# Sparse heads' attention weights: TensorE transposes replaced by DMA transposes of 16-bit planes, joined and weighted a head later

## The chip, the cores and the metric

The kernel runs on one core of a Trainium2 chip. The metric is the device time of one execution in microseconds (us). A core has five engines that work side by side, each through its own list of instructions in order: TensorE (PE in the profile; PEld is its loading of weights), VectorE (DVE), ScalarE (ACT), GpSimd (POOL) and SyncE (SP, which here issues DMAs). An engine that waits at one instruction holds up everything behind it in its list. Matrix products land in PSUM, eight banks of 128 partitions by 512 float32; everything else lives in SBUF.

## The reference

One block of a streaming encoder for 512 frames of 1024 channels, all in float32. A combined projection feeds two attention branches of 8 heads each and two gates; the branches are projected, gated, merged, put through an output projection and a layer norm; a gated feed-forward part follows. The change touches the sparse branch:

```python
def dsa_sequence(q, k, v, q_idx, k_idx, w_idx, rel_bias):      # in blocks of 128 queries
    dots = jnp.einsum('thd,sd->ths', qib, k_idx) * IDX_DIM ** -0.5
    score = jnp.einsum('th,ths->ts', wib, jax.nn.relu(dots))
    score = jnp.where(key_chunk[None, :] <= q_chunk, score, -jnp.inf)
    _, sel = lax.top_k(score, n_sel)                            # 128 keys for each query
    logits = jnp.einsum('thd,tnhd->htn', qb, k[sel]) * HEAD_DIM ** -0.5 + bias
    p = jax.nn.softmax(jnp.where(valid[None], logits, -jnp.inf), axis=-1)
    return jnp.einsum('htn,tnhd->thd', p, v[sel])
...
y_a, y_s = sparse branch, stick-breaking branch
merged = sigmoid(g_a + b0) * (y_a @ w_branch_dsa) + sigmoid(g_b + b1) * (y_s @ w_branch_sb)
```

The kernel doesn't gather keys. It computes the logits of all keys up to a query's block, adds a large penalty to those that were not chosen, and takes the softmax.

## The kernel before

Every product in float32 is made of three products in a reduced type, fp32r: a value is split into a high part (rounded to fp32r) and a low part (the rest), and high x high, high x low and low x high are summed. The weights are loaded by a `Stream` (one DMA of 512 KB on SyncE's queue per piece, three raw buffers); a piece is split by ScalarE (`whi`, L101) and by VectorE or GpSimd (`wlo`, L103).

The heads are taken in the order s0 to s7 (stick-breaking), then a0 to a7 (sparse). In pieces between the steps of the heads the main loop places "filler" matmuls, 15 at a time (`fill(GAP)`): projections of weights that will be wanted later, such as qa, ka (queries and keys of a pair of sparse heads), va (values of all sparse heads, four banks va_ps0 to va_ps3), gb and ga (gates), bs and ba (branch products). A scheduler takes the program with its own estimates of time and sets the final order on each engine; a list written once is then fixed. PSUM is shared by two pools of four banks: psA for the projections and branch products, psB for the heads' logits (l_ps, z_ps), transposes (tr_ps) and weighted values (av_ps).

A sparse head i goes through these steps. `dsa_head`: its bias window `win` comes by DMA (L474), GpSimd adds it to the scores' penalties in `bm` (L479, three blocks), TensorE makes the logits (l_ps, L490), VectorE adds `bm` and takes the row minimum into `lg` (L494, custom instruction), ScalarE takes the exponentials (L496), VectorE the reciprocals (L499) and scales `lg` by them (L502). `turn_weights`: TensorE transposes the ten 128 x 128 blocks of `lg` into three tr_ps banks (L410), ScalarE copies each bank to `pth` (high part, L414), VectorE subtracts to `ptl` (low part, L415). `weigh`: eight matmuls of the values with pth and ptl (L426: 512, 384, 256 and 128 columns, high and low), then ScalarE and VectorE add the two halves of the result (L431, L432), and every second head `finish_pair` splits it (L437, L438). The head after, i+1, has its `dsa_head` issued before head i is turned.

`proj_v` reads va_ps out: ScalarE the high parts (L252), VectorE the low parts (L253). Until all of va_ps is read out, nothing else fits into psA; the next user is the filler gb5 (lines 223 to 225).

The output projection further down, which the change leaves as it is, has a transpose of another make: ScalarE copies the two 16-bit planes of a float32 tile apart (L742), SyncE issues a DMA transpose for each (L743), ScalarE copies the planes back into one another (L750), and the high and low parts are made from that (L752, L753).

Of the kernel before, what the change touches and what calls it, by code (L numbers as in the profile page):

```python
# [11 lines left out]
F32 = mybir.dt.float32  # L12
# [32 lines left out]
OFF = {0: 0, 2: 128, 3: 512, 1: 1024}  # L45
ATT = 1280


def r32(ap):
    return ap.bitcast(F32)  # L50
# [67 lines left out]
def tile_block(ctx: ExitStack, tc: tile.TileContext, xT, xN, w_qi, w_ki, w_t, w_v, w_br, w_o, w_fi, w_fo,  # L118
# [86 lines left out]
    first = bp.tile([128, 512], F32, name="first")  # L205
# [139 lines left out]
    def idx_keys():  # L345
        ps = whole(proj_t("ki", M=72, bank=pa))
        kih = bp.tile([128, 512], F32R, tag="pt", bufs=8, name="kih")
        kil = bp.tile([128, 512], F32R, tag="pt", bufs=8, name="kil")
        wiT = bp.tile([8, 512], F32, tag="pt", bufs=8, name="wiT")
# [13 lines left out]
    def idx_scores():  # L363
        kih, kil, wi = index["k"]
        for j in (1, 2, 3):
            N = 128 * (j + 1)
            for h in range(H):
# [5 lines left out]
                rl = bp.tile([128, 512], F32, tag="pt", bufs=8, name="relu")  # L373
# [25 lines left out]

    def turn_weights(a):  # L400

        groups = (((0, 0),), ((1, 0), (3, 384)), ((2, 0),))
        pth, ptl = {}, {}
        for grp in groups:
# [7 lines left out]
            th = bp.tile([128, 512], F32R, tag="pt", bufs=8, name="pth")  # L412
            tl = bp.tile([128, 512], F32R, tag="pt", bufs=8, name="ptl")
            nc.scalar.activation(th[:, :width], ps[:, :width], AF.Copy)  # L414
            lows = nc.vector.tensor_sub(tl[:, :width], ps[:, :width], r32(th[:, :width]))  # L415
            for i, o in grp:
                pth[i] = th[:, o:o + 512 - 128 * i]
                ptl[i] = tl[:, o:o + 512 - 128 * i]
        return pth, ptl, lows.ins

    def weigh(pth, ptl, vt, h, ytmp):

        ps = pb("av_ps")
        seq = [(i, t) for i in range(NB) for t in (pth, ptl)]
        for n, (i, t) in enumerate(seq):
            nc.tensor.matmul(ps[:, 128 * i:512], vt[i][:, h].rearrange("p a d -> p (a d)"), t[i],  # L426
                             start=(n == 0), stop=(n == len(seq) - 1))
# [3 lines left out]
        nc.scalar.activation(tmp[own], ps[oth], AF.Copy)  # L431
        nc.vector.tensor_add(ytmp[own], ps[own], tmp[own])  # L432
# [39 lines left out]
    def dsa_head(q, k, h):  # L472
# [4 lines left out]
        for j in (1, 2, 3):  # L477
            N = 128 * (j + 1)
            nc.gpsimd.tensor_add(bm[:, OFF[j]:OFF[j] + N], win[:, 512 - N:512], score[j])  # L479
# [4 lines left out]
        for grp in ((3,), (0, 2), (1,)):  # L484
            ps = pb("l_ps")
            o = 0
            for j in grp:
# [4 lines left out]
                c = slice(OFF[j], OFF[j] + N)  # L492
                b = win[:, 384:512] if j == 0 else bm[:, c]
                nc.vector.tensor_tensor_reduce(out=lg[:, c], in0=ps[:, o:o + N], in1=b, scale=1.0, scalar=3.0e38,  # L494
# [642 lines left out]
```

## Time and profile before

| | us |
|---|---|
| median of 3 runs | 762.77 (762.73 to 762.90) |
| the profiled execution | 762.16 |
| span of its profile | 760.4 |
| TensorE busy | 748.6 (98%) |
| VectorE busy | 555.4 (73%) |
| ScalarE busy | 379.3 (50%) |
| GpSimd busy | 153.5 (20%) |
| TensorE clock granted, mean | 0.998 |

The profile is of one execution. The sparse heads' transposes lie between 206.1 and 321.4 us of it. In a row of a timeline the first number is the start in us from the span's start, the second the time from the first start to the last end, then engine, line, operation, output and inputs, partitions x elements, count; a bracket tells how long the engine sat idle before it and what released it. Rows of groups have the count, the busy time in us and the mean ns of one, then the idle time before it. Matmuls overlap, so the time of one row is longer than the step from its start to the next one's.

### The profile page before, as it was taken

To read this page: it belongs to the slowest core of one execution; us is meant where nothing else is said; L and a number is where in the kernel's file an instruction comes from. 1 tells how busy PE (TensorE), PEld (TensorE's weight loads), DVE (VectorE), ACT (ScalarE), POOL (GpSimd) and SP (SyncE) were. 2 spreads that over 40 slices of the span, in tenths; PEclk is the share of its full clock that TensorE was granted. 3 is DMA by queue.
4 is the path that set the end of the run, shared out by engine and by line. 5 is a ranking of instruction groups with operands and counts; after the bars stand their busy time and mean duration, and the time that the engine had idled before them with its cause. 6 is when DMAs were issued, how large, how long until landed. Compare 5 with 4: busy or idle time off the path is not lost.

```text
span 760.4 us, 9842 instructions
## 1 busy us (share of the span) xinstructions
PE 748.6 (98%) x3573; PEld 627.3 (82%) x3573; DVE 555.4 (73%) x905; ACT 379.3 (50%) x568; POOL 153.5 (20%) x160
## 2 busy tenths in 40 slices
PE   9999999999999999999999999999999999999995
PEld 7878888887888888888889888888888888888885
DVE  5569787799878585548765867766776768668995
ACT  5474756655574756835364633433443344346430
POOL 1002555426644210000111110111011101110012
PEclk9999999999999999999999999999999999999999
DMA  8445433232223324116942344544444444448632
GB/s 267 147 128 181 125 95 96 72 111 84 80 102 111 111 76 122 64 60 206 340 61 84 139 156 136 155 137 139 153 140 142 147 138 137 141 152 274 222 105 79
DMA packets 40448, 102.89 MB, mean 135 GB/s; under 512 B 10888, under 2 KB 11272, under 8 KB 40400
## 3 DMA queue, kind: packets, MB, share of 16 engines
q1 hardware_dynamic: 34672, 85.98, 35.4%
q0 software_dynamic: 3728, 11.04, 4.0%
q10 hardware_dynamic: 2000, 5.24, 2.8%
q8 instruction: 28, 0.46, 0.3%
q14 instruction: 20, 0.16, 0.1%
HBM read 88.59 MB, written 9.98 MB: 130 GB/s over the span
## 4 chain that ended last, share of the span: by engine, by line
PE 92%; DVE 5%; issue 1%; ACT 0%; POOL 0%; POOLq 0%; ACTq 0%; DVEq 0%
PE u_ps L774 5%; PE u_ps L776 5%; PE g_ps L774 5%; PE u_ps L775 5%; PE g_ps L776 5%; PE g_ps L775 5%; PE m L856 2%; PE m L854 2%; PE m L855 2%; PE av_ps L426 2%; PE ga_ps L224 2%; PE ga_ps L223 2%; PE ga_ps L225 2%; PE o_ps L704 2%; PE o_ps L703 2%; PE o_ps L705 2%
## 5 line engine op out<-in xcount | busy, mean ns | idle before, releaser
L101 ACT ACTIVATE whi<-raw 128x1024 fp32r<-128x1024 f32 (+1 forms) x124 | 124.1, 1001 | 169.5 <-PE g_ps L775 44.9
L103 DVE TENSOR_TENSOR wlo<-raw,whi 128x1024 fp32r<-128x1024 f32 (+1 forms) x105 | 120.0, 1144 | 41.3 <-ACT whi L101 40.5
L776 PE MATMUL u_ps<-x1h,wlo 128*128 128x512 f32 (+1 forms) x192 | 71.4, 372 | 0.0
L774 PE MATMUL u_ps<-x1h,whi 128*128 128x512 f32 (+1 forms) x192 | 71.3, 372 | 0.0
L775 PE MATMUL u_ps<-x1l,whi 128*128 128x512 f32 (+1 forms) x192 | 71.3, 371 | 0.0
L774 PE MATMUL g_ps<-x1h,whi 128*128 128x512 f32 (+1 forms) x184 | 69.9, 380 | 0.0
L775 PE MATMUL g_ps<-x1l,whi 128*128 128x512 f32 (+1 forms) x184 | 69.9, 380 | 0.0
L776 PE MATMUL g_ps<-x1h,wlo 128*128 128x512 f32 (+1 forms) x184 | 69.9, 380 | 0.0
L103 POOL TENSOR_TENSOR wlo<-raw,whi 128x1024 fp32r<-128x1024 f32 x19 | 45.8, 2412 | 34.5 <-ACT whi L101 34.4
L776 PEld LDWEIGHTS u_ps<-x1h,wlo 128*128 128x128 f32 x192 | 36.2, 188 | 6.3
L775 PEld LDWEIGHTS u_ps<-x1l,whi 128*128 128x128 f32 x192 | 36.2, 188 | 6.3
L774 PEld LDWEIGHTS u_ps<-x1h,whi 128*128 128x128 f32 x192 | 36.2, 188 | 6.2
L415 DVE TENSOR_TENSOR ptl<-tr_ps,pth 128x512 fp32r<-128x512 f32 (+1 forms) x48 | 27.9, 595 | 18.2 <-ACT pth L414 17.6
L776 PEld LDWEIGHTS g_ps<-x1h,wlo 128*128 128x128 f32 x184 | 34.6, 188 | 6.6
L775 PEld LDWEIGHTS g_ps<-x1l,whi 128*128 128x128 f32 x184 | 34.6, 188 | 6.5
L774 PEld LDWEIGHTS g_ps<-x1h,whi 128*128 128x128 f32 x184 | 34.6, 188 | 6.5
L797 DVE TENSOR_TENSOR t<-raw 128x512 f32<-128x512 f32 x11 | 7.6, 693 | 40.2 <-DMA raw<-in_w_fo_dram 40.2
L816 POOL MEMSET u<- 128x2 f32 x22 | 2.1, 98 | 143.7 <-ACT whi L101 99.9
L830 DVE TENSOR_TENSOR hF<-g_ps,c 128x512 f32<-128x512 f32 x22 | 15.1, 687 | 20.4 <-PE g_ps L776 20.4
L822 ACT ACTIVATE c<-c,cwt 128x512 f32<-128x512 f32 x22 | 16.0, 725 | 26.3 <-DVE c L821 26.1
L672 POOL TENSOR_TENSOR rstd<-rstd,mhalf 128x1 f32<-128x1 f32 x8 | 7.6, 951 | 106.0 <-DVE rstd L671 106.0
L414 ACT ACTIVATE pth<-tr_ps 128x512 fp32r<-128x512 f32 (+1 forms) x48 | 23.9, 520 | 9.8 <-PE tr_ps L410 6.8
(566 smaller groups left out, 2055.9 us busy)
## 6 DMA issues: line engine op xcount, KB each, us to landing
raw<-in_w_fi_dram SPq DMA_DIRECT2D x44, 512.0 KB, 3.3
raw<-in_w_t_dram SPq DMA_DIRECT2D x32, 512.0 KB, 3.4
raw<-in_w_fo_dram SPq DMA_DIRECT2D x26, 512.0 KB, 4.2
raw<-in_w_br_dram SPq DMA_DIRECT2D x8, 512.0 KB, 3.3
raw<-in_w_o_dram SPq DMA_DIRECT2D x8, 512.0 KB, 4.2
raw<-in_w_v_dram SPq DMA_DIRECT2D x7, 512.0 KB, 3.9
raw_b<-in_w_fo_dram SPq DMA_DIRECT2D x6, 512.0 KB, 4.2
s_t<-t POOLq DMA_DIRECT2D x11, 256.0 KB, 2.3
```

The source lines that it names most:

```text
L101: nc.scalar.activation(hi[:, :w], t[:, :w], AF.Copy)
L103: self.done[key] = eng.tensor_sub(lo[:, :w], t[:, :w], r32(hi[:, :w])).ins
L223: nc.tensor.matmul(ps[:M], wh[:, c], xh[k], start=(k == 0), stop=False)
L224: nc.tensor.matmul(ps[:M], wh[:, c], xl[k], start=False, stop=False)
L225: nc.tensor.matmul(ps[:M], wl[:, c], xh[k], start=False, stop=(k == KC - 1))
L414: nc.scalar.activation(th[:, :width], ps[:, :width], AF.Copy)
L415: lows = nc.vector.tensor_sub(tl[:, :width], ps[:, :width], r32(th[:, :width]))
L426: nc.tensor.matmul(ps[:, 128 * i:512], vt[i][:, h].rearrange("p a d -> p (a d)"), t[i], start=(n == 0), stop=(n == len(seq) - 1))
L774: nc.tensor.matmul(ps[:, c], wh[:, kc], x1h[:, k, c], start=(k == 0), stop=False)
L775: nc.tensor.matmul(ps[:, c], wh[:, kc], x1l[:, k, c], start=False, stop=False)
L776: nc.tensor.matmul(ps[:, c], wl[:, kc], x1h[:, k, c], start=False, stop=(k == KC - 1))
L822: nc.scalar.activation(c, c, AF.Gelu_apprx_tanh, bias=cwt[:, f, 3:4])
```

## The change

Sparse heads no longer use TensorE for their transposes. Stick-breaking heads still do.

- `send_planes`: once `lg` is scaled, ScalarE copies its odd 16-bit halves and VectorE its even ones (1280 each) into the memory of this head's own `bm`, which is read for the last time before that. SyncE issues two DMA transposes into `pl`. There is one buffer `pl` for all heads.
- `join_planes`: ScalarE copies the odd plane from `pl` into `back`, VectorE the even one; ScalarE makes `pth` of all 1280 columns, VectorE `ptl`. Both copies are issued after the next head's last exponential and last minimum.
- `weigh` comes a head later: head i is weighted after head i+1's logits are issued, just before head i+1's own planes are joined. The column order in `lg` is new (SOFF), so the transposed blocks of one block of keys lie three blocks apart and are read with a stride. Block 0's 512 columns take two pairs of matmuls (384 and 128), so ten matmuls a head.
- `pth` and `ptl` have one buffer of 1280 columns each now, for the stick-breaking heads too, where there were eight of 512 columns. Other tiles that used those eight move to other memory.

```diff
+SOFF = {1: 0, 0: 256, 2: 384, 3: 768}
...
-    first = bp.tile([128, 512], F32, name="first")
+    first = bp.tile([128, 512], F32, tag="pl", bufs=1, name="first")
...
-                rl = bp.tile([128, 512], F32, tag="pt", bufs=8, name="relu")
+                rl = bp.tile([128, 512], F32, tag=("keep", "av", "yt")[h % 3], bufs=2, name="relu")
...
+    def turned():
+        return (bp.tile([128, ATT], F32R, tag="th", bufs=1, name="pth"),
+                bp.tile([128, ATT], F32R, tag="tl", bufs=1, name="ptl"))
...
+    def halves16(t):
+        return t.bitcast(U16).rearrange("p (c two) -> p two c", two=2)
+
+    def send_planes(lg, bm):
+
+        src = halves16(lg)
+        own = bm[:, 0:ATT].bitcast(U16).rearrange("p (a c) -> p a c", a=2)
+        pl = bp.tile([128, 2, ATT // 128, 128], U16, tag="pl", bufs=1, name="pl")
+        nc.scalar.activation(own[:, 1], src[:, 1], AF.Copy)
+        nc.vector.tensor_copy(own[:, 0], src[:, 0])
+        for a in (0, 1):
+            nc.sync.dma_start_transpose(pl[:, a], own[:, a])
+        return pl
+
+    def join_planes(pl):
+
+        back = bp.tile([128, ATT], F32, tag="back", bufs=1, name="back")
+        got = pl.rearrange("p a b c -> p a (b c)")
+        nc.scalar.activation(halves16(back)[:, 1], got[:, 1], AF.Copy)
+        nc.vector.tensor_copy(halves16(back)[:, 0], got[:, 0])
+        th, tl = turned()
+        nc.scalar.activation(th, back, AF.Copy)
+        nc.vector.tensor_sub(tl, back, r32(th))
+        h, l = (t.rearrange("p (s c) -> p s c", c=128) for t in (th, tl))
+        parts = [(i, o, h[:, c], l[:, c]) for i, o, c in
+                 ((0, slice(128, 512), slice(0, 9, 3)), (0, slice(0, 128), slice(2, 3)),
+                  (1, slice(128, 512), slice(1, 9, 3)), (2, slice(256, 512), slice(5, 9, 3)),
+                  (3, slice(384, 512), slice(9, 10)))]
+        return parts
...
-        return lg
+        return send_planes(lg, bm), None, up.ins, low.ins
...
-        return sb_head(*args) if w == "s" else (dsa_head(*args),)
+        return sb_head(*args) if w == "s" else dsa_head(*args)
...
+    pair, joined = {}, None
     for i, (w, h) in enumerate(heads):
-        following = start_head(i + 1) if i + 1 < len(heads) else (None,)
+        following = start_head(i + 1) if i + 1 < len(heads) else ()
         fill(GAP)
...
+        else:
+            ends = following[2:]
+            if joined is not None:
+                added = values_of(*joined)
+                ends = ends or added
+            fill(GAP)
+            with tc.issue_after(ends[0]), tc.issue_after(ends[1]):
+                parts = join_planes(weights[0])
+            joined = parts, w, h
         fill(GAP)
         weights = following
+    fill(GAP)
+    values_of(*joined)
     fill(9999)
```

The order on VectorE around the read-out of va, before the change. The rows begin with the first sparse head's last scaling. lg_2102 and its mn_2103 are those of head a1; va0 to va3 are the values; ptl_2151 is a0's; ISA is the custom minimum.

```order
L502 TENSOR_SCALAR lg_1969<-lg_1969,rs_1972 128x512
L103 TENSOR_TENSOR wlo_36_2089<-raw_36_2086,whi_36_2088 128x1024
L494 ISA lg_2102,mn_2103<-l_ps_2111,win_2095 128x128
L494 ISA mn_2103 128x1
L432 TENSOR_TENSOR yst3_1917<-av_ps_2058,avt_2067 64x512
L494 ISA lg_2102,mn_2103<-l_ps_2120,bm_2098 128x256
L494 ISA mn_2103 128x1
L253 TENSOR_TENSOR va0_2207<-va_ps0_1945,va0_2207 128x8x64
L253 TENSOR_TENSOR va1_2210<-va_ps1_1946,va1_2210 128x8x64
L415 TENSOR_TENSOR ptl_2151<-tr_ps_2145,pth_2150 128x512
```

The same place on VectorE after the change, from a0's even plane on. lg_2075 is now head a1's, back_2144 is a0's joined tile, pl_1969 its landing buffer.

```order
L436 COPY bm_1937<-lg_1941 128x1280
L532 ISA lg_2075,mn_2076<-l_ps_2084,win_2068 128x128
L532 ISA mn_2076 128x1
L532 ISA lg_2075,mn_2076<-l_ps_2093,bm_2071 128x256
L532 ISA mn_2076 128x1
L469 TENSOR_TENSOR yst3_1889<-av_ps_2031,avt_2040 64x512
L104 TENSOR_TENSOR wlo_36_2062<-raw_36_2059,whi_36_2061 128x1024
L446 COPY back_2144<-pl_1969 128x1280
L532 ISA lg_2075,mn_2076<-l_ps_2084,bm_2071 128x384
L532 ISA mn_2076 128x1
L254 TENSOR_TENSOR va0_2206<-va_ps0_1917,va0_2206 128x8x64
L254 TENSOR_TENSOR va1_2209<-va_ps1_1918,va1_2209 128x8x64
```

The copy back from the landing buffer (L446) and a1's last minimum stand ahead of va0's low half, which stood right behind a1's third minimum; a0's low part, which was subtracted bank by bank, comes once and behind va1.

The order on GpSimd at the same place, before the change; bm_1965 and bm_2098 are the bias sums of a0 and a1, score3 the scores of the last block of queries.

```order
L103 TENSOR_TENSOR wlo_34_1952<-raw_34_1949,whi_34_1951 128x1024
L103 TENSOR_TENSOR wlo_35_2043<-raw_35_2040,whi_35_2042 128x1024
L479 TENSOR_TENSOR bm_1965<-win_1962,score3_370 128x512
L479 TENSOR_TENSOR bm_2098<-win_2095,score3_370 128x512
L475 MEMSET win_2256 64x64
```

And after the change, where bm_1937 is a0's, bm_2071 a1's.

```order
L104 TENSOR_TENSOR wlo_34_1924<-raw_34_1921,whi_34_1923 128x1024
L517 TENSOR_TENSOR bm_1937<-win_1934,score3_370 128x512
L517 TENSOR_TENSOR bm_2071<-win_2068,score3_370 128x512
L104 TENSOR_TENSOR wlo_35_2016<-raw_35_2013,whi_35_2015 128x1024
L513 MEMSET win_2166 64x64
```

The subtraction for the weights of gb5 (wlo_35) has moved from ahead of the two last bias sums to behind them.

On SyncE's queue, after the change, the DMA transposes stand between the loads (L72, weights) and the bias windows (L512); before the change the same loads stood there without them. pl_1969, pl_2103 and pl_2201 are a0's, a1's and a2's.

```order
L512 DMA win_2166<-s_win 128x512
L72 DMA raw_38_2218<-in_w_t_dram 128x1024
L438 DMA_TRANSPOSE pl_1969<-bm_1937 128x10x128 x2
L512 DMA win_2303<-s_win 128x512
L72 DMA raw_39_2266<-in_w_t_dram 128x1024
L512 DMA win_2492<-s_win 128x512
L72 DMA raw_40_2347<-in_w_t_dram 128x1024
L438 DMA_TRANSPOSE pl_2103<-bm_2071 128x10x128 x2
L72 DMA raw_41_2399<-in_w_t_dram 128x1024
L438 DMA_TRANSPOSE pl_2201<-bm_2169 128x10x128 x2
```

The loads of weights raw_39 to raw_41 now stand behind a head's transposes, which leave only when that head's planes are copied and the landing buffer has been read.

More of the change, by code (lines that the diff above doesn't have):

```diff
@@ L411, in turn_weights @@
                 width = max(width, o + 512 - 128 * i)
[L412 to L415, printed above, removed]
+            w = slice(base, base + width)
+            nc.scalar.activation(th[:, w], ps[:, :width], AF.Copy)
+            lows = nc.vector.tensor_sub(tl[:, w], ps[:, :width], r32(th[:, w]))
@@ L423, in weigh @@
+    def weigh(parts, vt, h, ytmp):
         ps = pb("av_ps")
-        seq = [(i, t) for i in range(NB) for t in (pth, ptl)]
-        for n, (i, t) in enumerate(seq):
-            nc.tensor.matmul(ps[:, 128 * i:512], vt[i][:, h].rearrange("p a d -> p (a d)"), t[i],
+        seq = [(i, o, t) for i, o, th, tl in parts for t in (th, tl)]
+        for n, (i, o, t) in enumerate(seq):
+            dst = ps[:, o] if len(t.shape) == 2 else ps[:, o].rearrange("p (s c) -> p s c", c=128)
+            nc.tensor.matmul(dst, vt[i][:, h].rearrange("p a d -> p (a d)"), t,
@@ L596, in tile_block, with values_of @@
     fill_until("qs1", "ks1")
+    def values_of(parts, w, h):
+        if h % 2 == 0:
+            pair[w] = bp.tile([128, 512], F32, tag="yt", bufs=2, name=f"y{w}t{h//2}")
+        fill_until(f"v{w}")
+        ends = weigh(parts, vals[w], h, pair[w])
+        if h % 2 == 1:
+            (ys if w == "s" else ya).append(finish_pair(pair[w], f"y{w}{h//2}"))
+        return ends
+    pair, joined = {}, None
     for i, (w, h) in enumerate(heads):
-        following = start_head(i + 1) if i + 1 < len(heads) else (None,)
+        following = start_head(i + 1) if i + 1 < len(heads) else ()
         fill(GAP)
-        pth, ptl, lows = turn_weights(weights[0])
-        if len(following) == 2:
-            with tc.issue_after(lows):
-                scan = sb_sticks(*following)
-            with tc.issue_after(scan):
-                select_some(ROUNDS[i])
-        fill(GAP)
-        if h % 2 == 0:
-            ytmp = bp.tile([128, 512], F32, tag="yt", bufs=2, name=f"y{w}t{h//2}")
-        fill_until(f"v{w}")
-        weigh(pth, ptl, vals[w], h, ytmp)
-        if h % 2 == 1:
-            (ys if w == "s" else ya).append(finish_pair(ytmp, f"y{w}{h//2}"))
+        if w == "s":
+            parts, lows = turn_weights(weights[0])
+            if len(following) == 2:
+                with tc.issue_after(lows):
+                    scan = sb_sticks(*following)
+                with tc.issue_after(scan):
+                    select_some(ROUNDS[i])
+            fill(GAP)
+            values_of(parts, w, h)
+        else:
[7 more added lines that the diff above has]
+            joined = parts, w, h
         fill(GAP)
         weights = following
+    fill(GAP)
+    values_of(*joined)
     fill(9999)
```

36 lines of the change are left out of this document (19 added, 17 removed).

## The prediction

> **What bounds the kernel now.** I read the page's busy shares first, then the chain that ended last, then TensorE's waits over the whole run, and only then the stage of the sparse heads, in windows.
>
> ```profile
> PE 748.6 (98%) x3573; PEld 627.3 (82%) x3573; DVE 555.4 (73%) x905; ACT 379.3 (50%) x568; POOL 153.5 (20%) x160
> PE 92%; DVE 5%; issue 1%; ACT 0%; POOL 0%; POOLq 0%; ACTq 0%; DVEq 0%
> PE idle_ps L200 <- DVE idle L197: 1.2, 1, 1.2
> PE dot_ps L371 <- ACT relu L374: 1.0, 1, 1.0
> PE va_ps L244 <- DVE ka1b L318: 0.9, 1, 0.9
> PE gb_ps L223 <- DVE va L253: 0.5, 1, 0.5
> 205.00:253.00 48.00, 47.47 (x236) 39.70 (x235) 37.83 (x72) 29.04 (x58) 20.84 (x19) 1.00 0.33 106
> ```
>
> TensorE bounds the kernel: it is busy for 98% and carries 92% of the chain, and its named waits add up to 3.6 us. So a matmul taken out is worth its full start-to-start time, as long as nobody makes TensorE wait. The last line is the stage from the first sparse transpose until head a4 (columns: window, length, then busy time of PE, PEld, DVE, ACT, POOL, then clock, DMA share, GB/s). VectorE works 37.83 of 48 us there, ScalarE 29.04. The cover is not wide: VectorE has some 10 us free in the very stage that the change loads. And the wait of gb_ps for va on VectorE shows the place where TensorE is already just caught.
>
> **a) The transposes that go: -8.7 us.**
>
> ```profile
> L410 PE MATMUL tr_ps<-ident,lg 128*128 128x128 f32 x80 | 12.3, 272 | 0.0
> 119.44 1.09 PE tr_ps L410 x10
> ```
>
> The first row counts them (80, ten a head); its 272 ns overlap one another and are not the price. The second is a piece of the chain: ten transposes advance it by 1.09 us, 0.109 each. 80 x 0.109 = 8.7; I leave 8.6 to 9.1 for their neighbours.
>
> **b) Narrower products: +0.2 us.** Block 0's 512 columns become 384 and 128, hi and lo, so 16 more matmuls.
>
> ```profile
> 319.31 0.34 PE L426 MATMUL av_ps<-pth,va 128*128 128x384 f32 x1
> 319.49 0.40 PE L225 MATMUL ga_ps<-xh,wlo 128*128 128x512 f32 x1
> 320.79 0.22 PE L426 MATMUL av_ps<-pth,va 128*128 128x128 f32 x1
> 320.85 0.27 PE L426 MATMUL av_ps<-ptl,va 128*128 128x128 f32 x1
> 210.88 0.39 PE L224 MATMUL gb_ps<-xl,whi 128*128 128x512 f32 x1
> 211.11 0.40 PE L225 MATMUL gb_ps<-xh,wlo 128*128 128x512 f32 x1
> ```
>
> Start to start 384 columns take 0.18 and 128 take 0.06, together 0.24; a 512-column product takes 0.23 (the last two rows). 16 x 0.01 = 0.2, between 0 and 0.5, as strided operands may cost a little and are not in this trace.
>
> **What the new path costs its engines.** The output projection of this kernel already sends 16-bit planes through DMA transposes, so most prices stand in the trace, for 1024 columns; the sparse heads have 1280, a factor of 1.25.
>
> ```profile
> L742 ACT ACTIVATE own<-r 128x1024 uint16<-128x1024 uint16 x6 | 6.0, 1047 | 8.2 <-DVE r L677 8.2
> L750 ACT ACTIVATE back<-got 128x1024 uint16<-128x1024 uint16 x6 | 7.7, 1358 | 5.5 <-DMA got<-own 5.5
> L743 SPq DMA_TRANSPOSE got<-own x6: 1233/1288/1353, 381.7 to 402.0; - x6
> DMA to landing us min/median/max: 3.1/3.2/4.9
> L752 ACT ACTIVATE x1h<-back x3: 1060/1061/1062, 389.2 to 406.6; 128x1024 fp32r<-128x1024 f32 x3
> L753 DVE TENSOR_TENSOR x1l<-back,x1h 128x1024 fp32r<-128x1024 f32 x3 | 3.7, 1221 | 1.6 <-ACT x1h L752 1.6
> L415 DVE TENSOR_TENSOR ptl<-tr_ps,pth 128x512 fp32r<-128x512 f32 (+1 forms) x48 | 27.9, 595 | 18.2 <-ACT pth L414 17.6
> L414 ACT ACTIVATE pth<-tr_ps 128x512 fp32r<-128x512 f32 (+1 forms) x48 | 23.9, 520 | 9.8 <-PE tr_ps L410 6.8
> ```
>
> Per head ScalarE gives up 23.9/16 = 1.49 us and takes on 1.31 (odd plane out), 1.70 (back) and 1.33 (pth): +2.85. VectorE gives up 27.9/16 = 1.74 and takes on ptl at 1.53 and two 16-bit copies of 1280. Such a copy is not in the trace of before. Half the subtraction's price, 0.76, is the low bound (half the bytes, and one source), the subtraction itself, 1.53, the high one; I take 1.1, the middle: +1.99 a head. SyncE's queue takes two issues of 1.29 x 1.25 = 1.6, one after the other; behind them stand the next loads of weights and of the bias window. A load behind them is up to 3.2 us later; with three raw buffers I cost that at nothing, and it would come to at most those 3.2 where a buffer is used as it lands.
>
> **c) The first join stands ahead of va's evacuation: +6.5 us.** On ScalarE and on VectorE the copies back for head a0 (L445, L446) now come before va0 is read out (L253, L254). gb5 needs the bank that this frees; the four va_ps fill all of that pool. VectorE's work while TensorE runs on becomes one serial walk: scaling, plane copies, two DMAs, copy back, va0.
>
> ```profile
> 204.57 0.17 DVE L499 RECIPROCAL rs<-sm 128x4 f32<-128x4 f32 x1
> 204.78 1.28 DVE L502 TENSOR_SCALAR lg<-lg,rs 128x128 f32<-128x128 f32 x4
> 201.40 2.53 POOL L479 TENSOR_TENSOR bm<-win,score 128x512 f32<-128x512 f32 x2 [0.36 <-DVE score L391]
> 240.69 2.52 POOL L103 TENSOR_TENSOR wlo<-raw,whi 128x1024 fp32r<-128x1024 f32 x1
> 212.91 3.81 POOL L479 TENSOR_TENSOR bm<-win,score 128x256 f32<-128x256 f32 x3 [1.08 <-DVE mn L494]
> 215.41 2.39 DVE L502 TENSOR_SCALAR lg<-lg,rs 128x128 f32<-128x128 f32 x4
> 237.98 5.51 DVE L502 TENSOR_SCALAR lg<-lg,rs 128x128 f32<-128x128 f32 x4
> 203.96 0.69 DVE L494 CUSTOM_DVE_ANT_0 lg<-l_ps,bm 128x512 f32<-128x512 f32 x1 [0.54 <-POOL bm L479]
> 209.80 1.29 DVE L253 TENSOR_TENSOR va<-va_ps,va 128x512 fp32r<-128x512 f32 x2 [1.21 <-ACT va L252]
> 210.55 0.50 PE L223 MATMUL gb_ps<-xh,whi 128*128 128x512 f32 x1 [0.53 <-DVE va L253]
> ```
>
> The scaling took 1.28 at 204.78 with GpSimd idle, 2.39 and 5.51 beside GpSimd's adds and subtractions; at 215.41 it ended 1.1 us after GpSimd's adds did (217.8 against 216.7). In the changed order GpSimd's wlo_35 stands behind the two bm adds, so it runs from 203.9 to 206.4, right beside this scaling (its first reader is gb5's third matmul, so its own lateness costs nothing). The scaling then ends at about 207.5 rather than 206.1. ScalarE's odd plane is out at 208.8; VectorE first does a1's pending minimum (0.69 and a short read), then its plane, until about 209.3. The even plane is the first sent: issue at 209.3, landing 3.2 later at 212.5, the odd one 1.6 behind, 214.1, and the copies back wait for both. Copy back 1.1, a1's next minimum 0.6, va0's low half 0.65 (1.29 for two), and gb5 starts at about 216.7 with its hop. Unhindered it would start at 210.55 - 0.53 (its old wait) - 1.09 (a0's transposes) + 0.81 (six l_ps products of a2 that now stand ahead, 512, 128 and 256 columns in pairs) = 209.7. Wait 7.0, less the 0.5 that it replaces: **+6.5**. Low bound: no GpSimd beside the scaling (-1.4), landing at 3.1, second issue at 1.3, copy at 0.76: +4.0. High bound: landing 4.9 (+1.7) and one copy held by GpSimd's next adds (+1.1): +9.3.
>
> What the Trainium skill says to this: "SBUF — State Buffer", section "SBUF: two separate sides", calls the port pair that VectorE shares with GpSimd an exclusive lock, so that one engine waits for the other's whole instruction. The rows at 204.78, 215.41 and 237.98 agree with it. By that rule the two plane copies could each also wait for a GpSimd instruction, 1 to 2.5 us more by the rows of L479 and L103, which would lead to the high end of c).
>
> **d) The later joins, a1 and a2, until a4: +3.5 us.** There is one landing buffer, so a head's DMAs wait for the join before it, and GpSimd's bias sums for the head after next wait until the planes have left their tile. VectorE carries for three heads 3 x 1.99 = 6.0 us more, ahead of the keys for the next pair:
>
> ```profile
> 249.62 0.69 DVE L318 TENSOR_TENSOR ka2b<-ka_ps,ka2b 64x512 fp32r<-64x512 f32 x1
> 253.35 0.96 PE L490 MATMUL l_ps<-ka2a,qa2a 128*128 128x512 f32 x5
> ```
>
> The keys end at 250.3 and TensorE uses them at 253.35, a margin of 3.0 us. TensorE also comes earlier, by 30 transposes, 3.3 us. With no slack used at all the stall would be 6.0 + 3.3 - 3.0 = 6.3; it is 0 if VectorE's 10 free us of the 48 take all of it. Those gaps lie partly where the new work cannot run (it waits for DMAs), so I take a little over the middle, 3.5. ScalarE's 3 x 2.85 = 8.6 fit into its 19 free us and are costed at nothing; without that cover they would come on top.
>
> **e) After the last head: +0.4 us.** a7's join hides behind ga5 and the first branch products, which no longer need it for more than 4 us; 0 to 1.5 if the landing is at its slowest.
>
> **Sum** against the profiled execution, 762.16 us (span 760.4 and 1.8 around it): -8.7 + 0.2 + 6.5 + 3.5 + 0.4 = +1.9, so 764.1. The median of the runs shown is 0.6 higher, 762.77, so the forecast is **764.7 us**.
>
> **The rivals.** *The clock falls in the pause* (0.13). For it:
>
> ```profile
> 1.18 4.02 PE idle_ps L200 x9
> ```
>
> At the start, after idling, nine matmuls take 4.02 us, 0.447 each, twice the 0.23 of later ones of 512 columns. If a pause of 7 us brings that state back, 4 us at half speed cost 2.1: 766.8. Against it: the page's clock row stands at its highest digit even there, and those matmuls may differ for their type. The Trainium skill, "TensorE: Matmul & The Clock Gate", section "HAM oscillation — how this bites in real kernels", tells of such a gate, with idle gaps above about 3.4 us closing it. No wait of this trace is that long; the longest has 1.2.
>
> *The joins break even* (0.27). c) stands but VectorE finds room for the joins, d) = 0: 764.7 - 3.5 = 761.2. For it: 10 free us on VectorE, and a stalled TensorE lets others catch up. Against it: the scaling of 5.51 us at 237.98 shows how little is sure there.
>
> *The transposes' time is kept* (0.17), the other side: VectorE and ScalarE reach va early because the planes leave at once, c) at its low bound 4.0, d) and e) nothing: -8.7 + 0.2 + 4.0 = -4.5, 758.3. It decides if gb5's first matmul starts before 214.2. For it: the uncontended scaling of 1.28; against it: GpSimd's subtraction, now placed beside that scaling.
>
> That the change leaves the transposes in place can be excluded: their instructions are gone from the order.
>
> **How the numbers follow.** The forecast has 0.43, on its own 762.8 to 766.6 (d from 1.6 to 5.4). A measurement here can tell about 0.2%, 1.5 us. Faster: all of the last rival and half of the break-even, 0.17 + 0.13 = 0.30. Same, 761.2 to 764.3: 0.14 of break-even and 0.15 of the forecast, 0.29. Slower: 0.28 and the clock's 0.13, 0.41. The range leaves out a little over half of the last rival and the worst of c) with the clock: 759.0 to 768.5.
>
> **What would show it.** No tr_ps in the sparse stage, and 8.7 us less busy time on TensorE; a wait of gb_ps for va of 5 to 9 us near 210, and in it VectorE waiting at L446 for the landing; l_ps of a4 waiting for the keys by 1 to 6 us; L540 of a0 near 2.7 us rather than 1.28; matmuls after the pause at 0.23, not 0.45. I am wrong if gb5 starts by 212, if VectorE's 16-bit copies take over 1.6, or if the time went where no wait is named here: weights that arrive late because the DMA issues of 1.6 us stand ahead of them in SyncE's queue.

## The result and the profile after

| | before | changed |
|---|---|---|
| median, us | 762.75 (762.51 to 762.90) | 767.64 (767.26 to 768.12) |
| the profiled execution, us | 762.16 | 767.37 |
| span of its profile, us | 760.4 | 765.6 |
| TensorE clock granted, mean | 0.998 | 0.993 |

The changed kernel is slower by 4.9 us, a ratio of 1.0066 with a 95% interval of 1.0053 to 1.0078. First the page's busy shares and the chain that ended last:

```profile
PE 745.0 (97%) x3509; PEld 622.2 (81%) x3509; DVE 568.1 (74%) x905; ACT 399.1 (52%) x568; POOL 155.5 (20%) x160
PE 60%; ACT 4%; DVE 2%; issue 1%; DMA 1%; POOL 0%; POOLq 0%; ACTq 0%; DVEq 0%
```

The 64 fewer matmuls are there (80 transposes less, 16 products more), but TensorE's busy time fell by 3.6 us only. Its part of the chain reads 60% where it was 92%, but the two can't be compared: followed back from the end, this chain stops at 242.4 us, so its shares add up to 68% and not to a whole. What it does show is that from 242 to 259 and from 295 to 331 us it lies on ScalarE, VectorE and DMAs. TensorE's waits say where (who waited, for whom, us in total, times, longest):

```profile
PE va_ps L245 <- DVE ka1b L319: 4.2, 1, 4.2
PE gb_ps L224 <- DVE va L254: 2.0, 1, 2.0
PE av_ps L463 <- ACT pth L448: 2.0, 1, 2.0
PE l_ps L528 <- DVE ka2a L318: 1.1, 1, 1.1
```

The dearest wait, 4.2 us for the keys ka1b, stands at 188 to 192 us, where the last stick-breaking heads run and no plane has been sent: the first DMA transpose comes at 210.7. Before, the same wait had 0.9. Two more things are in TensorE's timeline and in the windows around it (length, then busy us of PE, PEld, DVE, ACT, POOL, then clock, DMA share, GB/s):

```profile
192.32 0.76 PE L245 MATMUL va_ps<-whi,xh 128*128 128x512 f32 x1 [4.20 <-DVE ka1b L319]
192.89 0.63 PE L246 MATMUL va_ps<-wlo,xh 128*128 128x512 f32 x1
193.31 0.63 PE L247 MATMUL va_ps<-whi,xl 128*128 128x512 f32 x1
...
195.80 0.39 PE L245 MATMUL va_ps<-whi,xh 128*128 128x512 f32 x1
196.03 0.40 PE L246 MATMUL va_ps<-wlo,xh 128*128 128x512 f32 x1
```

```profile
192.00:195.40 3.40, 3.08 (x7) 2.48 (x8) 3.30 (x11) 0.83 (x3) 2.41 (x3) 0.54 0.00 0
195.40:200.00 4.60, 4.60 (x25) 3.93 (x24) 4.46 (x12) 2.06 (x5) 2.39 (x1) 0.97 0.00 0
332.00:335.40 3.40, 3.40 (x10) 2.63 (x10) 1.68 (x2) 0.00 (x0) 0.00 (x0) 0.53 0.18 43
```

After the wait the products start 0.43 us apart instead of 0.23, until 195.5; the granted clock of that window is 0.54. The same comes again at 332, just after the 2.0 us for pth. Each stretch lasts 3.41 us and does half its work, so each costs 1.7 us as long as TensorE has work all through it.

Taking the steps from one matmul's start to the next over the whole list, without the waits, the 5.2 us of span come apart as follows.

| | us |
|---|---|
| 80 transposes gone, by their own steps | -7.2 |
| narrower products (16 more, strided) | +0.7 |
| named waits, 12.5 in all after and 3.6 before | +8.9 |
| two stretches at half clock | +3.4 |
| not placed, among it shorter steps of the transposes' neighbours | -0.6 |

The 4.2 us. Here is VectorE's last scan (a helper of the stick-breaking heads), the keys behind it, and GpSimd's subtraction, before:

```profile
183.56 3.97 DVE L466 TENSOR_TENSOR_SCAN keep<-keep,first 128x128 f32<-128x128 f32 x4
182.31 2.40 POOL L103 TENSOR_TENSOR wlo<-raw,whi 128x1024 fp32r<-128x1024 f32 x1 [3.16 <-ACT whi L101]
188.85 0.69 DVE L318 TENSOR_TENSOR ka1b<-ka_ps,ka1b 64x512 fp32r<-64x512 f32 x1
```

and after:

```profile
185.06 5.11 DVE L504 TENSOR_TENSOR_SCAN keep<-keep,first 128x128 f32<-128x128 f32 x4
185.83 2.68 POOL L104 TENSOR_TENSOR wlo<-raw,whi 128x1024 fp32r<-128x1024 f32 x1 [4.63 <-ACT whi L102]
191.49 0.69 DVE L319 TENSOR_TENSOR ka1b<-ka_ps,ka1b 64x512 fp32r<-64x512 f32 x1
```

The order of the stage ahead of the sparse heads is another one: the scan starts 1.5 us later, and GpSimd's subtraction now falls into the middle of it, which makes it 1.1 us longer. Two earlier scans met a subtraction as well (all 32 together take 29.0 us instead of 25.2), and the last but one already starts 1.2 us late. So ka1b is 2.6 us later, and TensorE comes 0.7 us sooner. The only part of the change that touches this stage is the last one, the buffers.

The read-out of va, which the prediction walked through, looks like this after (VectorE, then TensorE):

```profile
206.29 0.18 DVE L537 RECIPROCAL rs<-sm 128x4 f32<-128x4 f32 x1 [0.88 <-ACT lg L534]
206.50 2.84 DVE L540 TENSOR_SCALAR lg<-lg,rs 128x128 f32<-128x128 f32 x4
209.88 0.82 DVE L436 COPY bm<-lg 128x1280 uint16<-128x1280 uint16 x1
215.78 0.90 DVE L446 COPY back<-pl 128x1280 uint16<-128x1280 uint16 x1 [1.02 <-DMA pl<-bm]
217.19 1.28 DVE L254 TENSOR_TENSOR va<-va_ps,va 128x512 fp32r<-128x512 f32 x2
```

```profile
214.94 1.07 PE L528 MATMUL l_ps<-ka1a,qa1a 128*128 128x512 f32 x6
218.03 0.47 PE L224 MATMUL gb_ps<-xh,whi 128*128 128x512 f32 x1 [2.01 <-DVE va L254]
```

From the reciprocal to gb5 it takes 11.7 us, one serial walk as foreseen. But TensorE is at gb5 at 216.0 only, not at 209.7: of these 6.3 us it lost 5.0 at ka1b, in the wait (3.3 more than before) and in the clock (1.7). So it waits 2.0 us.

### The profile page after: what moved, and what is told of

It is laid out like the page before. It is cut to its first block, busy times and chain, and to the rows that moved or that the text cites. A ratio compares the mean times of both kernels' runs of the same rounds, so it can differ in the third digit from the quotient of the medians.

```text
span 765.6 us, 9753 instructions
## 1 busy us (share of the span) xinstructions
PE 745.0 (97%) x3509; PEld 622.2 (81%) x3509; DVE 568.1 (74%) x905; ACT 399.1 (52%) x568; POOL 155.5 (20%) x160
## 4 chain that ended last, share of the span: by engine, by line
PE 60%; ACT 4%; DVE 2%; issue 1%; DMA 1%; POOL 0%; POOLq 0%; ACTq 0%; DVEq 0%
PE u_ps L830 5%; PE u_ps L829 5%; PE g_ps L830 5%; PE u_ps L831 5%; PE g_ps L829 5%; PE g_ps L831 5%; PE m L909 2%; PE m L910 2%; PE m L911 2%; PE o_ps L760 2%; PE o_ps L759 2%; PE o_ps L758 2%; PE ba_ps L709 1%; PE ba_ps L710 1%; PE ba_ps L711 1%
## 5 line engine op out<-in xcount | busy, mean ns | idle before, releaser
L104 DVE TENSOR_TENSOR wlo<-raw,whi 128x1024 fp32r<-128x1024 f32 (+1 forms) x105 | 122.2, 1165 | 37.2 <-ACT whi L102 36.6
L517 POOL TENSOR_TENSOR bm<-win,score 128x256 f32<-128x256 f32 (+2 forms) x24 | 28.4, 1210 | 26.6 <-DMA pl<-bm 17.9
L504 DVE TENSOR_TENSOR_SCAN keep<-keep,first 128x128 f32<-128x128 f32 (+3 forms) x32 | 29.0, 962 | 0.0
```

The costliest lines, as they stand in the source:

```text
L104: self.done[key] = eng.tensor_sub(lo[:, :w], t[:, :w], r32(hi[:, :w])).ins
L504: scan = nc.vector.tensor_tensor_scan(rev, rev, first[:, 512 - N:512][:, ::-1], 0.0, op0=ALU.mult, op1=ALU.max)
L517: nc.gpsimd.tensor_add(bm[:, SOFF[j]:SOFF[j] + N], win[:, 512 - N:512], score[j])
```

## Experiments

Edits are to the changed kernel where nothing else is said. The kernel before, run beside each, had medians of 762.3 to 762.6 us. A ratio is to it, with its 95% interval.

**1. The buffers alone.** The kernel before with the changed kernel's buffers only; the sparse heads stay on TensorE and are weighted at once. (kih, kil, wiT and `first` move as in the change; they are not shown.)

```diff
-            th = bp.tile([128, 512], F32R, tag="pt", bufs=8, name="pth")
-            tl = bp.tile([128, 512], F32R, tag="pt", bufs=8, name="ptl")
+        th, tl = turned()
...
-                rl = bp.tile([128, 512], F32, tag="pt", bufs=8, name="relu")
+                rl = bp.tile([128, 512], F32, tag=("keep", "av", "yt")[h % 3], bufs=2, name="relu")
```

> The kernel before with only the change's buffers: pth and ptl single, relu tiles on keep, av and yt, the scan constant under another tag; sparse heads are turned by TensorE and weighted at once, as before. Theory A (the time was lost ahead of the sparse heads: with these buffers the scheduler orders that stage anew, VectorE's scans fall under GpSimd's subtractions, TensorE waits 4.2 us at va for ka1b and then runs 3.4 us at half clock): the same 4.2 us wait of va_ps for ka1b and the same clock dip here, about 767.5 us. Theory B (the joins of the sparse heads cost it, as forecast): no such wait, 762.5 to 763.5 us.

775.58 us, 1.0175 (1.0161 to 1.0189): 13 us slower than before, and 8 us more than expected. TensorE's waits:

```profile
PE gb_ps L223 <- DVE va L253: 5.1, 1, 5.1
PE va_ps L244 <- DVE ka1b L318: 4.2, 1, 4.2
```

The 4.2 us are there without a single plane, and half-clock stretches too: 10.2 us of them, of which TensorE worked 7.4, so 3.7 are lost. What these two waits grew by (7.9), smaller waits (0.9) and the clock make 12.5 of the 12.8 us by which the span is longer. 4.8 of it is at ka1b. Another 6.8 is at gb5, where VectorE is late with va although no join stands ahead of it (4.6 of waiting, 2.2 of clock); that was not expected. With the same buffers the plane path is then worth 775.6 - 767.6, 8 us of gain.

**2. The changed kernel with TensorE's transposes.** Heads weighted a head later, as in the change.

```diff
-                parts = join_planes(weights[0])
+                parts = turn_weights(weights[0], SOFF)[0]
```

> The changed kernel with the sparse heads' transposes back on TensorE, still weighted a head later and with the changed buffers: no planes, no DMA transposes, no joins. Theory A: the va wait and the clock dip stay; the transposes come back (+7.6), the narrower products (-0.8) and the waits of gb5, ka2a and a7 with the second clock dip (-1.5, -1.1, -2.0, -1.7) go: 767.6 + 0.5 = about 768 us. Theory B: without joins about 763 us.

775.62 us, 1.0169 (1.0155 to 1.0183), as much as the first and 8 us more than expected. Weighting a head later neither costs nor gains in sum, though not term by term: the wait for va is 3.8 here and not 5.1, and 13.7 us run at half clock, not 10.2. So the 8 us belong to the planes, but not all of it to the transposes: the clock costs 5.4 us here and 3.4 in the change.

**3. The first join behind the read-out of va.**

```diff
-            with tc.issue_after(ends[0]), tc.issue_after(ends[1]):
+            fill_until("va")
+            with tc.issue_after(ends[0]), tc.issue_after(ends[1]), tc.issue_after(read_out["va"]):
```

> The changed kernel with the first sparse head's join issued behind the read-out of va on ScalarE and VectorE. If the join's place makes gb5 wait (term c of the prediction): the wait of gb_ps for va falls from 2.0 to 0.5 us or less, and the time by 1.5 to 2, to about 766 us. Rival: VectorE is only behind, so the time comes back as a longer wait of l_ps for ka2a (1.1 us now) and the kernel stays at 767.6 us.

765.70 us, 1.0041 (1.0029 to 1.0054), 1.9 less than the change.

```profile
...
PE av_ps L465 <- ACT pth L450: 2.2, 1, 2.2
...
PE gb_ps L224 <- DVE va L256: 0.7, 1, 0.7
PE l_ps L530 <- DVE ka2a L320: 0.3, 1, 0.3
```

The wait for va falls by 1.3 and the one for the keys of a4 by 0.8, together 2.1. So the join's place does cost TensorE time at gb5, about a third of what the prediction put there. The 4.2 us for ka1b stand. (The profiled execution, at 766.18 us one of the longer ones, has 6.8 us at half clock from 190.5 where the change's has 3.4, at a place that the edit doesn't touch.)

**4. How long a pause lowers the clock.** Not the reference's work: runs of 36 to 46 equal products of 512 columns, and between them a pause made by a chain of VectorE additions of growing length.

```diff
+    for n, (widths, count) in enumerate(PAUSES):
...
+        for k in range(count):
+            nc.tensor.matmul(ps, lhs, x, start=(k == 0), stop=(k == count - 1))
...
+        for w in widths:
+            nc.vector.tensor_add(d, src, raw)
...
+        nc.vector.tensor_scalar(lhs, src[:, 0:128], 2e-3, None, op0=ALU.mult)
```

> Not the reference's work: TensorE multiplies in runs of 36, 41 and 46 products of 512 columns, and between the runs it waits for a chain of 0 to 8 additions on VectorE, pauses of about 0.8 to 6 us, each length three times; the output is a copy of the last operand. Theory C (a pause of about 2 us can halve the clock for 3.4 us, depending on where it falls in a fixed grid of time): all pauses over some length are followed by products at 0.43 us, those about 2 us only sometimes, and the granted clock shows 0.5 for 3.4 us each time. Rival (only pauses over 3.4 us do it; the dip at 332 us has another cause): pauses of 2 to 3 us are never followed by slow products.

TensorE's timeline, with the pause in the bracket; 36 products at 0.23 take 8.4 us, 41 take 9.6, and a stretch at half clock adds 1.7:

```profile
35.16 10.08 PE L133 MATMUL ps<-x,lhs 128*128 128x512 f32 x36 [1.77 <-DVE lhs L140]
47.74 8.45 PE L133 MATMUL ps<-x,lhs 128*128 128x512 f32 x36 [2.50 <-DVE lhs L140]
59.42 10.07 PE L133 MATMUL ps<-x,lhs 128*128 128x512 f32 x36 [3.23 <-DVE lhs L140]
...
140.46 9.60 PE L133 MATMUL ps<-x,lhs 128*128 128x512 f32 x41 [1.77 <-DVE lhs L140]
```

The same pause of 1.77 costs 1.7 us once and nothing another time; 2.50 likewise. Counted over the run, 0.38 and 1.14 never lowered the clock (three of each), 1.77 did once in three, 2.50 twice in three, 3.23 and longer always. The starts of all products and the times at which the granted clock changes, taken one by one, explain most of this: every change of clock lies on one grid of 3.413 us, and between products a slow stretch is one or two of its cells long. Idleness counted from these starts, less 0.23 for the last product, is 0.16 longer than the bracket. Over this run and the profiles of all the kernels here, between their first products and their last, a cell with 1.91 us of idleness or less was never followed by one at half clock, and one with 2.04 or more always. Between the two it went either way: the first and the last pause of 1.77, both 1.93 by this count and both within one cell, differ, and 2.02 in experiment 5 cost nothing. A slow cell with 0.61 us of idleness or more was followed by another slow one, with 0.57 or less it was not. In the changed kernel the 2.01 us ahead of gb5 fell across two cells and cost no clock; the 1.97 us at 329 fell into one and did. The Trainium skill, "TensorE: Matmul & The Clock Gate", section "HAM oscillation — how this bites in real kernels", puts the gap that closes the gate above 3.4 us. The runs differ: 3.4 us is the cell, and a pause that the profile shows as 1.77 can be enough; the measurement decides.

**5. GpSimd taken off the scan.** The low half of va's third weight piece is made by VectorE, so no subtraction of GpSimd meets the scan.

```diff
-POOL_LO += [f"va{g}" for g in range(4)]
+POOL_LO += [f"va{g}" for g in (0, 1, 3)]
```

> The changed kernel, but the low half of the weights va2 is subtracted on VectorE and not on GpSimd. In the changed kernel that subtraction ran from 185.8 to 188.5 us, and the last stick-breaking head's scan took 5.35 us beside it, against 3.2 undisturbed. Theory A (VectorE loses time while GpSimd's subtraction runs, which makes ka1b late): the scan takes 3.2 us, VectorE does 1.2 us more itself, ka1b is about 1 us earlier, the va wait falls from 4.2 to about 3.2 us and the time by 1 to 2 us, to 766 us. Rival (the scan is slow for another reason): the scan stays at 5.35, va waits 5.4 us, about 769 us.

768.04 us, 1.0074 (1.0059 to 1.0089): no gain, where 766 was expected. The scan's row, then the waits:

```profile
185.21 2.96 DVE L504 TENSOR_TENSOR_SCAN keep<-keep,first 128x128 f32<-128x128 f32 x4
```

```profile
PE l_ps L528 <- DVE ka2a L318: 3.2, 1, 3.2
PE va_ps L245 <- DVE ka1b L319: 3.0, 1, 3.0
...
PE av_ps L463 <- DVE ptl L420: 1.4, 1, 1.4
```

The cause of the long scan is shown: 2.96 us where it had 5.11, with GpSimd idle. The Trainium skill, "SBUF — State Buffer", section "SBUF: two separate sides", calls the port pair that the two engines share an exclusive lock, held for a whole instruction; the trace agrees, as the scan took 2.15 us more beside a subtraction of 2.68. The time is not gained, since VectorE does the subtraction itself now and all that it saves ahead is waited for later: the keys of a4 cost 3.2 instead of 1.1. The clock gives nothing either: the wait of 3.0 for ka1b spreads over two cells and costs none, and the 3.2 behind it cost two, at 257.0 to 263.9, as many as the change has.

**6. The last head on TensorE**, beside the edit of 3.

```diff
+BY_PE = (7,)
...
-        return send_planes(lg, bm), None, up.ins, low.ins
+        return lg if h in BY_PE else send_planes(lg, bm), None, up.ins, low.ins
```

> The kernel with a0's join behind va's read-out, and the last sparse head, a7, transposed by TensorE as before. Theory: a7's landing is the tail that no filler covers (2.2 us of wait for pth and 1.7 us of half clock behind it); ten transposes come back at 1.0: 765.7 - 2.2 - 1.7 + 1.0 = about 762.8 us. Rival: the wait for the last products stays, as ScalarE and not the DMA is late: 765 to 767 us.

762.78 us, 1.0004 (0.9995 to 1.0013), equal to before and 2.9 less than experiment 3. In its profile the 2.2 us for pth are gone and two stretches of 3.4 us at half clock, which cost 2.5; ten transposes are back (1.1), and the waits for va and the keys have 1.0 more. That makes -2.6, and the span fell by 3.2. Of the two stretches, one stood behind the wait for pth (at 330.4, 1.7); the other, at 190.5 (0.8, as TensorE waited through a part of it), stood ahead of all that this edit touches, so that it is gone is chance. Without it the tail is worth 2.2 + 1.7 - 1.1 = 2.8 us. It is shown as a cost of its own, but not as one of the DMA's latency alone. In the changed kernel a7's second plane, issued at 321.4, landed at 325.2, and the two engines took it up 2.2 and 3.6 us later, behind other work of theirs:

```profile
327.42 1.64 ACT L445 ACTIVATE back<-pl 128x1280 uint16<-128x1280 uint16 x1
328.79 0.87 DVE L446 COPY back<-pl 128x1280 uint16<-128x1280 uint16 x1
```

The edit takes away both the landing and this delay; no run separates them.

**7. The relu tiles' new place alone**, in the kernel before.

```diff
-                rl = bp.tile([128, 512], F32, tag="pt", bufs=8, name="relu")
+                rl = bp.tile([128, 512], F32, tag=("keep", "av", "yt")[h % 3], bufs=2, name="relu")
```

> The kernel before with one change: the indexer's relu tiles rotate over keep, av and yt; pth and ptl keep their eight buffers. Theory A1 (fewer buffers for pth and ptl reorder the stage): no va wait over 1 us, about 762.5 us. Theory A2 (the relu tiles reorder it): the 4 us wait and the clock dips come, 768 us or more.

763.16 us, 1.0009 (0.9999 to 1.0018). TensorE's waits are those of before, 0.9 for ka1b and 0.5 for va. The relu tiles aren't it.

**8. Other rounds of the key selection** (the table that says how many rounds of VectorE's top-k search follow each stick-breaking head), on top of 6, meant to give the keys ka1b more time.

```diff
-ROUNDS = 3, 3, 4, 5, 5, 6, 6
+ROUNDS = 5, 5, 5, 5, 4, 4, 4
```

> As the run with a7 on TensorE, and the top-k rounds behind the stick-breaking heads spread 5, 5, 5, 5, 4, 4, 4 and not 3, 3, 4, 5, 5, 6, 6. Theory A (VectorE is saturated between 152 and 200 us, and has room before): ka1b comes before TensorE needs it, the va wait falls under 1 us and its clock dip goes, -3.3 and -1.7 to -3.4: about 757 us, below the kernel before. Rival: the rounds moved forward make the stick-breaking heads late instead, TensorE waits there: 762 us or more.

764.59 us, 1.0024 (1.0014 to 1.0035), a miss. The wait for ka1b fell to 3.2 but the one for va rose from 1.4 to 3.6, and three cells ran at half clock instead of one.

**9. The old buffers for the stick-breaking heads.** They get a pool of seven 512-column buffers, closed ahead of the first join; pth, ptl and back of the joins get that memory. (There were eight before.)

```diff
+    kc, kp = open_pool("kp")
...
+                th = kp.tile([128, 512], F32R, tag="pt", bufs=7, name="pth")
+                tl = kp.tile([128, 512], F32R, tag="pt", bufs=7, name="ptl")
...
+                close(kc)
+                late_pool["c"], late_pool["jp"] = open_pool("jp", reuse_waits="tile")
```

> The changed kernel with the stick-breaking stage's own buffers restored: pth and ptl in three tiles each, relu, kih, kil and wiT in one ring of seven 512-column buffers, in a pool that is closed before the first join, whose memory the joins then use. Everything on the sparse heads' side is the change's. Theory A (the buffers cost the time, the DMA transposes gain): the va wait falls from 4.2 to about 1 us and has no clock dip; left are the gain (-7.6 + 0.8), the wait behind a7's landing (+2.0), its dip (+1.7) and some 0.5 to 1 at ka2a or gb5: 762.4 - 3 = about 759.5 us, 757.5 to 761. Theory B (the joins cost it): va's wait is only moved, gb5 then waits 5 to 7 us for va as forecast, 764 us or more.

766.00 us, 1.0043 (1.0029 to 1.0056). More than was expected.

```profile
PE l_ps L536 <- DVE mn L540: 2.4, 1, 2.4
PE l_ps L536 <- DVE ka2a L320: 2.3, 1, 2.3
PE av_ps L471 <- ACT pth L456: 1.7, 1, 1.7
...
PE va_ps L247 <- DVE ka1b L321: 0.9, 1, 0.9
```

Ahead of the sparse heads all is as before: the wait for ka1b has 0.9 again, and the 32 scans take 25.2 us as before, against 29.0 in the changed kernel. TensorE is therefore at gb5 at 211.6, and it doesn't wait there: in this order VectorE reads va0 out ahead of the first join,

```profile
210.80 0.69 DVE L256 TENSOR_TENSOR va<-va_ps,va 128x512 fp32r<-128x512 f32 x1
214.48 0.92 DVE L454 COPY back<-pl 128x1280 uint16<-128x1280 uint16 x1 [0.41 <-DMA pl<-bm]
```

and the later joins meet a TensorE that is on time: 4.7 us of waits for VectorE stand in the next heads, and two cells at half clock cost 3.2. VectorE's and GpSimd's rows there:

```profile
226.54 3.53 DVE L548 TENSOR_SCALAR lg<-lg,rs 128x128 f32<-128x128 f32 x4
240.11 5.18 DVE L548 TENSOR_SCALAR lg<-lg,rs 128x128 f32<-128x128 f32 x4
```

```profile
226.70 3.09 POOL L525 TENSOR_TENSOR bm<-win,score 128x256 f32<-128x256 f32 x3 [4.47 <-DMA pl<-bm]
238.57 3.63 POOL L525 TENSOR_TENSOR bm<-win,score 128x256 f32<-128x256 f32 x3 [8.79 <-DMA pl<-bm]
```

GpSimd's bias sums wait for the planes to leave their memory (8.79 us once). They then run beside VectorE's scaling, the second time with a subtraction of 2.43 right behind them, and the scaling takes 3.53 and 5.18 us, against the 1.28 of the row shown before with GpSimd idle.

**10. Experiments 3, 6 and 9 together.**

> The run with the old buffers, and the two mends of the runs before: a0's join behind va's read-out, and a7 transposed by TensorE. Theory A: no wait over 1.5 us and no clock dip left, -6.8 for seven heads' transposes and the narrower products with some 0.5 of new waits: about 756.5 us, faster than the kernel before. Theory B: 762 us or more.

759.74 us, 0.9964 (0.9951 to 0.9976): faster than both kernels, by 2.6 us and by 7.9. One wait of note is left, of av_ps for yat on VectorE (1.9 us, at 234), with one cell at half clock. Together these are 3.6; it missed its expectation, 756.5, by 3.2.

**11. pth and ptl in single buffers, the rest of the old ones left**, in the kernel before. The relu tiles keep their tag here, with four buffers instead of eight.

```diff
-            th = bp.tile([128, 512], F32R, tag="pt", bufs=8, name="pth")
+        th, tl = turned()
...
-                rl = bp.tile([128, 512], F32, tag="pt", bufs=8, name="relu")
+                rl = bp.tile([128, 512], F32, tag="pt", bufs=4, name="relu")
```

> The kernel before with pth and ptl as the change has them, one buffer of 1280 columns each (kih and kil in them too), and the relu tiles still in a ring of their own, of four and not eight; sparse heads on TensorE and weighted at once. Theory A1 (the single pth and ptl reorder the stage ahead of the sparse heads): a va wait of 3 us or more with its clock dip, 766 us or more. Rival (it takes the relu tiles and these together, or the order falls as it falls): the va wait stays near 1 us, about 763 us.

770.12 us, 1.0097 (1.0082 to 1.0112). The wait for ka1b has 4.0 us, and the last scan lies beside GpSimd's subtraction again:

```profile
187.61 5.12 DVE L471 TENSOR_TENSOR_SCAN keep<-keep,first 128x128 f32<-128x128 f32 x4
```

With 7 this narrows the cause to pth and ptl and what moved with them (kih and kil into their buffers, wiT, first), but for the four relu buffers.

**12. Two blocks of each scaling moved to ScalarE**, on top of 10, to take VectorE's scaling from beside GpSimd's sums.

```diff
-            nc.vector.tensor_scalar(lg[:, c], lg[:, c], rs[:, j:j + 1], None, op0=ALU.mult)
+            if j in (2, 3):
+                nc.scalar.activation(lg[:, c], lg[:, c], AF.Copy, scale=rs[:, j:j + 1])
+            else:
+                nc.vector.tensor_scalar(lg[:, c], lg[:, c], rs[:, j:j + 1], None, op0=ALU.mult)
```

> The run with both mends and the old buffers, and the two larger blocks of each sparse head (384 and 512 columns) scaled by the reciprocals on ScalarE and not on VectorE. Theory (VectorE's scaling, stretched from 1.28 to 2.4 to 5.5 us by GpSimd's bias sums that the landing releases, is what makes the later joins late): the scaling on VectorE takes under 1.5 us, the 1.9 us wait at a1's products and its dip go, about 756.5 us. Rival (ScalarE is now the late one): the wait stays or moves to pth, 759.5 us or more.

759.83 us, 0.9969 (0.9958 to 0.9981), the same as 10 and the time that the rival gave. The 1.9 us for yat are gone, with the cell at half clock; in their place stand

```profile
PE l_ps L539 <- DVE ka2a L323: 2.0, 1, 2.0
PE gb_ps L227 <- DVE va L259: 1.3, 1, 1.3
```

```profile
240.62 3.16 DVE L554 TENSOR_SCALAR lg<-lg,rs 128x128 f32<-128x128 f32 x2
```

In seven heads VectorE's part of the scaling took 0.55 us. In a3, the head ahead of the late keys ka2a, it still met GpSimd and took 3.16. So the run doesn't settle what that scaling costs.

## Why the prediction came out as it did

The direction was right and 767.64 lies in the range, but the time came by another road. **The step that failed is one that the sum doesn't have: the fourth part of the change, the buffers.** The change's list names it, and the prediction gave it no price; it took the stage ahead of the sparse heads as it was. Alone it costs 13 us (experiment 1), 4.8 of them at ka1b and 6.8 at gb5; in the changed kernel it is 3.3 us of waiting and 1.7 us of clock at ka1b.

With this the terms c) to e) were, taken together, too dear for the kernel as it is. Beside the same buffers the planes gain 8 us, where the sum had a loss of 1.9. The two errors, about 13 and 10, nearly cancel. That the time came within 2.9 us of the forecast is luck. Nearest to the prediction's own frame, where the buffers cost nothing, is experiment 9: +3.7 us, against the +1.9 of the sum. But it is no confirmation, since the order there has no join ahead of va and c) is nothing; the time goes to the later waits and to 3.2 of clock. The two costs don't add: 13 and 3.7 would make 16.7, and the change has 4.9. Whoever is held up ahead waits less later.

- **a)** -7.2 by the transposes' own steps, where -8.7 stood. The products right behind them take longer steps too, and with these ten transposes cost 1.1 in experiment 6, so the price of 0.109 each is not shown to be wrong.
- **b)** +0.7 where +0.2 stood, above its bound of 0.5. With a) and what is not placed that is -7.1, where -8.5 stood.
- **c)** The mechanism holds: the walk took 11.7 us (12.1 predicted), the scaling of a0 2.84 (2.7), and gb5 did wait for va behind the join. What was mis-sized is the other end, TensorE's arrival: 216.0 instead of 209.7. So the term was +1.5 and not +6.5, and moving the join gave 1.9 back (experiment 3). No run has the walk against a TensorE that is on time.
- **d)** +1.1 at a4's keys where +3.5 stood. Where TensorE is on time it is 2.3 for the keys and 2.4 for a minimum (experiment 9), within the bounds of 0 to 6.3. The reason given, the joins' load on VectorE, is likely a part of it. Another is the scaling beside GpSimd's work, its sums above all, which the landing buffer delays into it: 5.18 us instead of 1.28 ahead of those keys. How much of the waits each makes is not shown, as experiment 12 left the scaling of a3 beside GpSimd.
- **e)** +2.0 and 1.7 of clock, where +0.4 stood with a bound of 1.5. The join hides behind ga5 alone: in TensorE's order the branch products come behind a7's first product, so it ran out of work 2.0 us before pth was there. The landing was not at its slowest (3.8 us); the plane then stood for 2.2 and 3.6 us until ScalarE and VectorE came to it, a term that the prediction didn't have. By experiment 6 the tail is worth 2.8.
- **The prices of the new path** were near. The groups of the plane buffer, pl:

```profile
L438 SPq DMA_TRANSPOSE pl<-bm x16: 1255/1349/1997, 210.7 to 321.4; - x16
L445 ACT ACTIVATE back<-pl x8: 1642/1653/1697, 214.4 to 327.4; 128x1280 uint16<-128x1280 uint16 x8
L446 DVE COPY back<-pl x8: 868/902/911, 215.8 to 328.8; 128x1280 uint16<-128x1280 uint16 x8
DMA to landing us min/median/max: 3.5/3.8/5.2
```

A plane copy on VectorE took 0.82 out and 0.90 back (1.1 taken for each), the copy back on ScalarE 1.65 (1.70), an issue 1.35 (1.6), a landing 3.8 (3.2).

- **The rival of the clock** was right in its mechanism and wrong in its place. It was priced for a pause of 7 us at gb5. It came after pauses of 4.2 and 2.0 elsewhere, for 3.41 us each. The argument against it, that the page's clock row stands at its highest digit, fails: a slice of that row is 19 us long, and a stretch of 3.4 at half clock still leaves it above nine tenths.
- **The two other rivals** had d) at nothing, or c) at its low bound of 4.0 with d) and e) at nothing. Measured, c) was 1.5 and d) 1.1, nearer to them than to the forecast; the time went the other way all the same, by the buffers and the tail.
- **The named signs**: no transposes in the sparse heads, the scaling at 2.84, VectorE waiting at L446 for the landing (1.0) and the keys of a4 (1.1) were right; 8.7 us less busy time was wrong (3.6), mostly as products at half clock count as busy longer (3.4); the wait of 5 to 9 us at gb5 was 2.0; the time that went where no wait was named was not in SyncE's queue but ahead of the stage.

**What stays open.** Why single buffers for pth and ptl lead the scheduler to an order in which GpSimd's subtractions meet the scans was not settled: other tiles moved with them, and the relu tiles had four buffers. No run separates those. The stretched scan is not all of the wait either: with it gone, 3.0 of the 4.2 us stood (experiment 5, where VectorE had the subtraction to do). Nor is it known how the edits of experiment 10 share its gain over 9.

## What to carry to other kernels

Where a scheduler sets the order, a buffer that is merged or moved is an edit to every stage that uses it: compare the order of the stages that the change doesn't name, too, and price that before the new path. Take the cost of a wait from when the waiting engine really arrives, not from the old trace; a delay ahead pays for one behind. On a kernel bound by TensorE, count a wait near 2 us as up to 3.7, since the clock may fall after it, and give the last item of a pipeline the path with the shortest latency even if the others take the cheap one.

## What the hardware showed that was not expected

- The clock changes on a grid of 3.413 us. It fell by half for a cell after every one with 2.04 us or more of idleness, after none with 1.91 or less, and either way between. So the same pause of 2.50 us costs 1.7 us or nothing, by where it falls on the grid. The grid isn't tied to the program's start: the first change to full clock comes 5.9 us into the profile of the kernel before and 4.6 us into that of the changed one, though the first product starts at 1.18 in both.
- Five executions of experiment 3 spread over 764.8 to 766.6 us, and the granted clock goes with it: 0.995 and 0.996 in the two fastest, 0.991 to 0.993 in the others. So the grid is a likely cause. It isn't the only one: experiment 7 spreads over 762.4 to 764.1 us at 0.996 to 0.998, the lowest in the fastest.
- Scans on VectorE stretch beside a GpSimd subtraction, 5.11 us against 2.96 for four, and scalings beside GpSimd sums, up to 5.18 against 1.28.
- A 16-bit copy of 1280 columns is faster on VectorE (0.82 us out, 0.90 back) than on ScalarE (1.27 out, 1.65 back), though both read or write every second half-word on one side.
